# A fourth seven-product unit per column group in a gated MLP, with part of the weight preparation done by adding transfers

## The chip, the cores and the metric

The kernel runs on one core of one Trainium2 chip. The metric is the device time of one execution in microseconds (us). A core has a matrix engine (TensorE, "PE" in the profile, its weight loads "PEld"), VectorE ("DVE"), ScalarE ("ACT"), GpSimd ("POOL") and SyncE ("SP"). Transfers are issued from the queues of SP, POOL or ACT and carried by 16 DMA engines.

## The reference

One layer of an encoder over 256 rows of width 2048, all in float32: four mixers side by side, a cross-attention to 256 memory rows, and a gated MLP of width 5632, which is where nearly all of the change lies.

```python
def swiglu(h, w_gate_up, w_down):
    gate, up = jnp.split(h @ w_gate_up, 2, axis=-1)
    return (jax.nn.silu(gate) * up) @ w_down

# in reference():
    x = x + mix @ w_out[l]
    x = x + cross_attention(rms_norm(x, norm_g[l, 1]), mem_n, w_xq[l], w_xkv[l], w_xo[l])
    x = x + swiglu(rms_norm(x, norm_g[l, 2]), w_gate_up[l], w_down[l])
return rms_norm(x, final_norm_g)
```

`w_gate_up` is 2048 x 11264 and `w_down` 5632 x 2048.

## The kernel before

**Precision.** Every large product is made of three: an operand is split into a high part, rounded to the matrix engine's shorter float32 format (`F32R`), and a low part, the rest. High x high, high x low and low x high are added up in PSUM (`part`, lines 489 to 493, whose three matmuls are the profile's lines L490, L491 and L492).

**The stream of weights** (`class Stream`). All weights come in one host-packed tensor `W`, in the order of use, in slabs of 128 x 2048 (1 MB). `raw` issues a slab's load on SP's queue (L134) into one of three raw buffers; gate and up have a fourth (`rawx`). `make` prepares the next half slab of 1024 columns: `split` has ScalarE copy it into `wh` (L154) and VectorE subtract that copy from it into `wl` (L155). `look` prepares as many halves ahead as there are buffers (`free`): three pairs of `wh` and `wl` in the pool `wp`, and two more in `wp2` during gate and up, five in all, one of them being in use. When TensorE has used a half up, `drop` gives its buffer back.

**Gate and up** (`gate_up`). The 5632 columns are worked off in eleven groups j of 512 gate and 512 up columns. The depth 2048 is cut into eight slabs i per group, each two blocks of 128 deep by the two column sets. A plain slab is 24 matmuls of 512 columns: two blocks, two column sets, two halves of the 256 rows, three products each. A "seven-product" slab (`seven`, `sevens`, `unit`) treats the same data as a 2 x 2 by 2 x 2 block product and forms it with seven block products in place of eight (Strassen's scheme in Winograd's form), so 21 matmuls. For that, sums and differences of the blocks are needed: those of the activations are formed once, before the first group (`left`, in the tiles `sh` and `sl`), and those of the weights for each slab by VectorE in the raw buffer (`make`, L187). Such a slab is prepared in four parts:

- part 0: split of 512 columns, then one subtraction over 1024;
- part 1: split of 1024, then two sums over 512;
- parts 2 and 3: splits of 1024 of what now stands in the raw buffer.

Of four accumulators, p1, p5, p6 and p7, `combine` makes the unit's share of the four results after the group's last unit; `finish` adds the plain part, applies the SiLU and the product in the next group, and `store_turned` transposes the gated product (L520) and stores it to the DRAM tensor `hidden` in four transfers per half of the rows (L525), from which `fetch` (L936) later reloads it for the product with `w_down`. In the same stage `turn` transposes the residual (L1069), stores it to `xrows` (L1072), and loads it back in row order.

Numbers such as "slab 2" or "unit 5" below are i in a group; "second half" is part 1 of a plain slab.

**Order.** Side work runs as generators (`Background`): `poll` steps one on when its time has come and an account of VectorE's work (`owed`, increased by `bg.dve` and paid off by `bg.pe`) is low. The program is written in one order, but each engine's queue is put in order by a planner ahead of time, by priority and by its own estimate of when operands are ready. `keep_place` (`keep` in the stream) pins instructions behind the one that precedes them in the program on the same engine. In `make` the parts of seven-product slabs are pinned, those of plain slabs are not. An engine runs its queue strictly in that order.

At the start the keys of the cross-attention are made (`mixers`, the loop over `w_xkv`): the first pass makes 1024 columns in step with the arriving input, two more passes 512 each; all their turned stores go through `store_turned(..., True)`, which pins the transposes.

Of the kernel before, what the change touches and what calls it, by code (L numbers as in the profile page):

```python
# [18 lines left out]
ALU = mybir.AluOpType  # L19
# [30 lines left out]

def sevens(j):

    return (1, 3, 5) if j else (5,)


FORMED = 6
# [50 lines left out]
PI_LO = float(np.nextafter(np.float32(math.pi), np.float32(0)))  # L107


class Stream:  # L110


# [32 lines left out]
                return pool  # L145
        return None

    def split(self, pool, at, r, edges):

        nc = self.nc  # L150
        wh, wl = (pool.tile([P, 1088], F32R, name=t, tag=t) for t in ("wh", "wl"))
        wh, wl = wh[:, at:at + 1024], wl[:, at:at + 1024]
        for a, b in zip(edges, edges[1:]):
            nc.scalar.copy(wh[:, a:b], r[:, a:b])  # L154
            nc.vector.tensor_tensor(out=wl[:, a:b], in0=r[:, a:b], in1=wh[:, a:b].bitcast(F32), op=ALU.subtract)  # L155
        self.bg.dve(edges[-1], len(edges) - 1)
        self.items.append((pool, wh, wl))

    def make(self):

        nc, (slab, part) = self.nc, self.todo
        n = 16 * slab + 8 * part
        if n >= NBLK - HELD:
            parts = [(self.places.pop(0)) for _ in range(2)]
            r = self.raw(slab)[:, part * 1024:part * 1024 + 1024]
            for a, (wh, wl) in zip((0, 512), parts):
                nc.scalar.copy(wh, r[:, a:a + 512])
                nc.vector.tensor_tensor(out=wl, in0=r[:, a:a + 512], in1=wh.bitcast(F32), op=ALU.subtract)
            self.bg.dve(1024, 2)
            self.items.append((None, parts))  # L170
            self.todo = (slab + part, 1 - part)
            return True
        pool = self.free(slab)
        if pool is None:
            return False
        raw = self.raw(slab)
        at = 48 if any(a <= n < b for a, b in ROWS) else 8
        r = raw[:, part % 2 * 1024:part % 2 * 1024 + 1024]
        if not seven(slab):
            mark = len(nc.cur_bb.bb.instructions)  # L180
            self.split(pool, at, r, [0, 256, 512, 1024] if n == 0 else [0, 512, 1024] if n == 8 else [0, 1024])
            if DOWN <= slab < DOWN + 2 * AHEAD:
                self.keep(mark)
            self.todo = (slab + part, 1 - part)
            return True
        mark = len(nc.cur_bb.bb.instructions)
        op = lambda out, a, b, what=ALU.subtract: nc.vector.tensor_tensor(out=out, in0=a, in1=b, op=what)  # L187
        self.split(pool, at, r, [0, 512] if part == 0 else [0, 1024])
        b11, b12, b22, b21 = (raw[:, a:a + 512] for a in range(0, 2048, 512))
        if part == 0:  # L190
            blk = raw.rearrange("p (b c) -> p b c", b=4)
            op(r.rearrange("p (b c) -> p b c", b=2), blk[:, 0:3:2, :], blk[:, 1:2, :].to_broadcast([P, 2, 512]))
            self.bg.dve(1024)
        elif part == 1:
            op(b22, b22, b11, ALU.add)
            op(b21, b21, b22)
            self.bg.dve(1024, 2)
        self.keep(mark)
        self.todo = (slab + part // 3, (part + 1) % 4)
        return True  # L200
# [87 lines left out]
class Block:  # L288
# [223 lines left out]
                    self.bg.poll()  # L512
        return ps

    def store_turned(self, to, u, src, keep=False):

        nc = self.nc
        self.bg.dve(src.shape[1])
        mark = self.mark()
        nc.vector.transpose(u, src)  # L520
        if keep:
            self.keep_place(mark)
        to = to.rearrange("(b f) t -> f b t", f=32)
        for a in range(4):
            nc.gpsimd.dma_start(to[:, :, 32 * a:32 * a + 32],  # L525
                                u[32 * a:32 * a + 32, :].rearrange("f (b t) -> f b t", t=32))


# [46 lines left out]
    def mixers(self):  # L575
# [77 lines left out]
        with tc.tile_pool(name="mid", bufs=1) as mid:  # L653
            self.dgp = mid
            gl = Gla(self, mid)
            with tc.tile_pool(name="hyp", bufs=1) as hyp, tc.tile_pool(name="k2", bufs=8) as k2:
                hy = Hyena(self, hyp, k2)

                mem0 = hy.piece()[:, 0:R + 16]
                nc.sync.dma_start(mem0, self.t["mem0"])  # L660
                self.bg.add(prepare(mid))

                for cols in ([0, 512], [1024], [1536]):
                    first = dict(parts=[[k] for k in range(KT)], before=start_m) if len(cols) > 1 else {}
                    for c, ps in zip(cols, self.gemm_rows("w_xkv", cols, h, **first)):
                        for r in range(2):
                            self.store_turned(self.kd[c:c + 512, r * P:(r + 1) * P], hy.piece(), ps[r][:, :], True)
                    if first:
                        for k in range(0, KT, 4):
                            self.load_x(k, 4)  # L670
                for hd in range(4):
                    for r, p in enumerate(self.gemm_rows("w_xkv", [D + hd * 512], h, start_x if hd == 3 else rows.append)[0]):
                        for c in range(2):
                            v, o = self.tmp(), (2 * hd + r) * 512 + c * R
                            nc.scalar.activation(v, p[:, c * R:(c + 1) * R], AF.Copy, scale=self.rcm[:, r:r + 1])
                            nc.gpsimd.dma_start(self.vd[:, o:o + R], v)
                self.bg.drain()

                def ev_u(i, p):
                    hy.feed(i, self.merge(p))  # L680
                    if i == 4:
                        self.bg.add(hy.convs())

                self.gemm("w_in", [UH + i * P for i in range(12)], h, ev_u)
                for r, p in enumerate(self.gemm_rows("w_in", [512], h, lambda k: k or low_rank())[0]):
                    nc.scalar.copy(gl.v[r], p)
                self.gemm("w_in", [256, 384, 0, 128], h, lambda i, p: gl.feed(i, self.merge(p)))
                self.gemm("w_in", scols[0:NSC], h, ev_s, narrow=True)
                self.bg.drain()
# [261 lines left out]
    def gate_up(self, sw, gp, f):  # L951
# [8 lines left out]

        def left():

            for i in (5, 1, 3):
                t = [self.tmp() for _ in range(2)]
                for x, k in zip(t, (2 * i, 2 * i + 1)):
                    nc.scalar.activation(x, self.resk(k), AF.Copy, scale=self.gvec(V_NG + 32, k))
# [37 lines left out]
        def finish(j, cs, s):  # L1004
# [9 lines left out]
            for r in range(2):  # L1014
                g, h = s[r]
                u = gp.tile([P, 512], F32, name="u", tag="u", bufs=2)
                self.stt(h, h, box["col"][:, r:r + 1], g, ALU.mult, ALU.mult)
                yield SOON
                self.store_turned(self.ff[j * 512:(j + 1) * 512, r * P:(r + 1) * P], u, h)
                yield SOON  # L1020
            self.stored.append(j)

# [39 lines left out]
    def turn(self):  # L1062
# [3 lines left out]
        for i in range(16):  # L1066
# [2 lines left out]
            nc.vector.transpose(u, self.resk(i))  # L1069
            for a in range(4):  # L1070
                c = i * P + 32 * a
                nc.gpsimd.dma_start(to[:, :, c:c + 32], u[32 * a:32 * a + 32, :].rearrange("t (b f) -> t b f", f=32))  # L1072
            yield 4.0
        for c in range(4):
            for r in range(2):
# [783 lines left out]
```

## Time and profile before

| | |
|---|---|
| time, median of 3 runs | 1458.29 us (1456.57 to 1458.53) |
| the profiled execution | 1457.18 us, its span 1455.3 us |
| PE busy | 1440.2 us, 99% |
| DVE busy | 1192.2 us, 82% |
| ACT busy | 844.1 us, 58% |
| POOL busy | 172.2 us, 12% |
| moved by transfers | 307.16 MB, 211 GB/s on the mean |

The span is that of one execution taken by the hardware profiler; the profiled time contains 1.9 us around it. Matmuls overlap: one of 512 columns lasts 389 ns in the records, and the next starts before it has ended, so the spacing of starts and not the duration counts. In a row of groups the columns are the line and engine, the operation, what it writes and reads, the count, the busy time with the mean in ns, and the idle time before it with what ended it. In the DMA rows the last number is the median from issue to landing. Gate and up take about 755 to 1210 us of the span.

### The profile page before, as it was taken

What the parts mean: (1) busy time and instruction counts of PE and PEld (TensorE: products, weight loads), DVE (VectorE), ACT (ScalarE), POOL (GpSimd) and SP (SyncE); (2) the same over time, 40 slices, a digit from 0 to 9 for tenths busy, and PEclk for the clock granted to TensorE, in tenths of its full rate; (3) what the DMA queues carried; (4) which work ended last, traced back from release to release, by engine and by line L of the source; (5) the groups of instructions that cost most, each with busy time, mean ns of one, the idle gap of its engine ahead of it and who ended that gap; (6) DMA issues with size and microseconds to landing.
All of it is one profiled execution on the core that took longest, in us unless ns stands there. A gap on an engine that the chain in (4) does not pass through costs nothing.

```text
span 1455.3 us, 19732 instructions
## 1 busy us (share of the span) xinstructions
PE 1440.2 (99%) x7219; PEld 1217.8 (84%) x7219; DVE 1192.2 (82%) x1748; ACT 844.1 (58%) x1252; POOL 172.2 (12%) x294
## 2 busy tenths in 40 slices
PE   9999999999999999999999999999999999999997
PEld 7788888888899888888888888888888888788886
DVE  6577768777868867877778999999999997988875
ACT  6466665456646656665555565555555654655554
POOL 0220100000000001110003334112111112100000
PEclk9999999999999999999999999999999999999999
DMA  9885654444535555555556767656667656545554
GB/s 351 283 314 192 229 193 169 174 158 167 206 122 203 204 200 203 185 174 177 199 191 221 252 234 245 241 191 244 234 228 248 207 198 235 216 183 200 224 203 145
DMA packets 57394, 307.16 MB, mean 211 GB/s; under 512 B 9774, under 2 KB 11471, under 8 KB 25681
## 3 DMA queue, kind: packets, MB, share of 16 engines
q1 hardware_dynamic: 45920, 281.11, 54.2%
q0 software_dynamic: 10944, 24.14, 5.5%
q8 instruction: 56, 0.92, 0.2%
q10 hardware_dynamic: 432, 0.66, 0.1%
q14 instruction: 42, 0.34, 0.1%
HBM read 291.71 MB, written 14.16 MB: 210 GB/s over the span
## 4 chain that ended last, share of the span: by engine, by line
PE 96%; DVE 2%; ACT 1%; issue 0%; DMA 0%; SPq 0%; ACTq 0%; DVEq 0%
PE pg L439 19%; PE pg L490 13%; PE pg L491 13%; PE pg L492 13%; PE pg L440 10%; PE pm L490 7%; PE pm L492 7%; PE pm L491 7%; PE pm L1360 1%; DVE wl L155 1%; PE pg L436 1%; PE pg L437 1%; PE pm L890 1%; PE pm L863 1%; ACT wh L154 0%
## 5 line engine op out<-in xcount | busy, mean ns | idle before, releaser
L154 ACT CAST wh<-raw 128x1024 fp32r<-128x1024 f32 (+1 forms) x589 | 589.2, 1013 | 473.1 <-PE pg L492 147.3
L155 DVE TENSOR_TENSOR wl<-raw,wh 128x1024 fp32r<-128x1024 f32 (+1 forms) x589 | 681.8, 1176 | 183.7 <-ACT wh L154 178.0
L439 PE MATMUL pg<-act,wh 128*128 128x512 f32 x1104 | 387.5, 393 | 0.0
L440 PE MATMUL pg<-act,wl 128*128 128x256 f32 x1216 | 340.7, 280 | 0.0
L490 PE MATMUL pg<-wh,act 128*128 128x512 f32 (+1 forms) x689 | 269.6, 392 | 2.3 <-DVE k L520 2.0
L491 PE MATMUL pg<-wl,act 128*128 128x512 f32 (+1 forms) x689 | 268.8, 390 | 1.2 <-DVE wl L155 1.1
L492 PE MATMUL pg<-wh,act 128*128 128x512 f32 (+1 forms) x689 | 268.8, 390 | 0.0
L439 PEld LDWEIGHTS pg<-act,wh 128*128 128x128 f32 x1104 | 207.4, 188 | 45.0
L440 PEld LDWEIGHTS pg<-act,wl 128*128 128x128 f32 x1216 | 228.5, 188 | 0.8 <-DVE wl L155 0.5
L490 PEld LDWEIGHTS pg<-wh,act 128*128 128x128 f32 x689 | 129.7, 188 | 31.0 <-ACT dgh L410 2.4
L491 PEld LDWEIGHTS pg<-wl,act 128*128 128x128 f32 x689 | 129.6, 188 | 29.2 <-DVE wl L155 2.5
L492 PEld LDWEIGHTS pg<-wh,act 128*128 128x128 f32 x689 | 129.7, 188 | 27.3
L491 PE MATMUL pm<-wl,act 128*128 128x512 f32 x318 | 123.7, 389 | 0.0
L492 PE MATMUL pm<-wh,act 128*128 128x512 f32 x318 | 123.7, 389 | 0.0
L490 PE MATMUL pm<-wh,act 128*128 128x512 f32 x318 | 123.6, 389 | 0.0
L187 DVE TENSOR_TENSOR raw<-raw 128x1024 f32<-128x1024 f32 x129 | 111.8, 866 | 3.0
L525 POOL DMA_DIRECT2D hidden<-u x88 | 56.8, 653 | 164.6 <-DVE u L520 141.9
L492 PEld LDWEIGHTS pm<-wh,act 128*128 128x128 f32 x318 | 59.7, 188 | 12.5
L491 PEld LDWEIGHTS pm<-wl,act 128*128 128x128 f32 x318 | 59.7, 188 | 12.4
L490 PEld LDWEIGHTS pm<-wh,act 128*128 128x128 f32 x318 | 59.7, 188 | 12.4
L1072 POOL DMA_DIRECT2D xrows<-tmp x64 | 37.0, 585 | 183.5 <-DVE rc L321 126.6
L936 POOL DMA_DIRECT2D tmp<-hidden x44 | 24.5, 560 | 141.2 <-DVE f L317 73.0
(353 smaller groups left out, 1773.1 us busy)
## 6 DMA issues: line engine op xcount, KB each, us to landing
raw<-in_W SPq DMA_DIRECT2D x246, 1024.0 KB, 4.9
raw<-in_W SPq DMA_DIRECT2D x11, 512.0 KB, 7.5
hidden<-u POOLq DMA_DIRECT2D x88, 64.0 KB, 4.4
tmp<-hidden POOLq DMA_DIRECT2D x44, 128.0 KB, 4.2
res<-in_xT SPq DMA_DIRECT2D x8, 512.0 KB, 7.5
k<-in_mem SPq DMA_DIRECT2D x8, 256.0 KB, 6.5
k<-in_x SPq DMA_DIRECT2D x8, 256.0 KB, 7.7
keys<-k POOLq DMA_DIRECT2D x32, 64.0 KB, 5.3
```

Of the source, the lines that this page charges most:

```text
L154: nc.scalar.copy(wh[:, a:b], r[:, a:b])
L155: nc.vector.tensor_tensor(out=wl[:, a:b], in0=r[:, a:b], in1=wh[:, a:b].bitcast(F32), op=ALU.subtract)
L187: op = lambda out, a, b, what=ALU.subtract: nc.vector.tensor_tensor(out=out, in0=a, in1=b, op=what)
L436: self.nc.tensor.matmul(p[:, 0:R], wh, slot[:, 0:R], start=start, stop=False)
L439: self.nc.tensor.matmul(p[:, :], wh, slot[:, :], start=start, stop=False)
L440: self.nc.tensor.matmul(p[:, 0:R], wl, slot[:, 0:R], start=False, stop=stop)
L490: self.nc.tensor.matmul(p, hi, wh, start=start, stop=False)
L491: self.nc.tensor.matmul(p, hi, wl, start=False, stop=False)
L492: self.nc.tensor.matmul(p, lo, wh, start=False, stop=stop)
L525: nc.gpsimd.dma_start(to[:, :, 32 * a:32 * a + 32], u[32 * a:32 * a + 32, :].rearrange("f (b t) -> f b t", t=32))
L936: self.nc.gpsimd.dma_start(m[k], self.ff[k * P:(k + 1) * P, :])
L1072: nc.gpsimd.dma_start(to[:, :, c:c + 32], u[32 * a:32 * a + 32, :].rearrange("t (b f) -> t b f", f=32))
```

## The change

Four things change.

1. In groups j = 1 to 10, slab 4 becomes a fourth seven-product slab: units are now slabs 1, 3, 4 and 5, so three follow each other. `left` forms the activation sums for slab 4 too. Group 0 keeps its single unit.
2. In those groups the second half of each plain slab (0, 2, 6, 7) is split in another way (`added`): ScalarE writes the negated rounding of the raw half into `wl`, a transfer on POOL's queue adds the raw half to it, and ScalarE copies the rounding into `wh`. VectorE takes no part.
3. The stores of the gated product and of the turned residual go on SP's queue and not on POOL's.
4. In the first pass of the keys the transposes are no longer pinned; in the other passes they are.

```diff
--- before.py
+++ after.py
@@ -50,7 +50,7 @@
 
 def sevens(j):
 
-    return (1, 3, 5) if j else (5,)
+    return (1, 3, 4, 5) if j else (5,)
 
 
 FORMED = 6
@@ -105,6 +105,12 @@
 TWO_PI_3 = float(2 * math.pi - 6.28125 - float(np.float32(2 * math.pi - 6.28125)))
 MAGIC = float(np.float32(1.5 * 2 ** 23))
 PI_LO = float(np.nextafter(np.float32(math.pi), np.float32(0)))
+
+
+def added(slab):
+
+    j, i = divmod(slab - GU // 16, 8)
+    return j >= 1 and slab < DOWN and i not in sevens(j)
 
 
 class Stream:
@@ -145,11 +151,17 @@
                 return pool
         return None
 
-    def split(self, pool, at, r, edges):
+    def split(self, pool, at, r, edges, added=False):
 
         nc = self.nc
         wh, wl = (pool.tile([P, 1088], F32R, name=t, tag=t) for t in ("wh", "wl"))
         wh, wl = wh[:, at:at + 1024], wl[:, at:at + 1024]
+        if added:
+            nc.scalar.mul(wl, r, -1.0)
+            nc.gpsimd.dma_start(wl, r.bitcast(F32R), accum_op=ALU.add)
+            nc.scalar.copy(wh, r)
+            self.items.append((pool, wh, wl))
+            return
         for a, b in zip(edges, edges[1:]):
             nc.scalar.copy(wh[:, a:b], r[:, a:b])
             nc.vector.tensor_tensor(out=wl[:, a:b], in0=r[:, a:b], in1=wh[:, a:b].bitcast(F32), op=ALU.subtract)
@@ -178,7 +190,7 @@
         r = raw[:, part % 2 * 1024:part % 2 * 1024 + 1024]
         if not seven(slab):
             mark = len(nc.cur_bb.bb.instructions)
-            self.split(pool, at, r, [0, 256, 512, 1024] if n == 0 else [0, 512, 1024] if n == 8 else [0, 1024])
+            self.split(pool, at, r, [0, 256, 512, 1024] if n == 0 else [0, 512, 1024] if n == 8 else [0, 1024], part == 1 and added(slab))
             if DOWN <= slab < DOWN + 2 * AHEAD:
                 self.keep(mark)
             self.todo = (slab + part, 1 - part)
@@ -512,7 +524,7 @@
                     self.bg.poll()
         return ps
 
-    def store_turned(self, to, u, src, keep=False):
+    def store_turned(self, to, u, src, keep=False, queue=None):
 
         nc = self.nc
         self.bg.dve(src.shape[1])
@@ -522,7 +534,7 @@
             self.keep_place(mark)
         to = to.rearrange("(b f) t -> f b t", f=32)
         for a in range(4):
-            nc.gpsimd.dma_start(to[:, :, 32 * a:32 * a + 32],
+            (queue or nc.gpsimd).dma_start(to[:, :, 32 * a:32 * a + 32],
                                 u[32 * a:32 * a + 32, :].rearrange("f (b t) -> f b t", t=32))
 
 
@@ -664,7 +676,7 @@
                     first = dict(parts=[[k] for k in range(KT)], before=start_m) if len(cols) > 1 else {}
                     for c, ps in zip(cols, self.gemm_rows("w_xkv", cols, h, **first)):
                         for r in range(2):
-                            self.store_turned(self.kd[c:c + 512, r * P:(r + 1) * P], hy.piece(), ps[r][:, :], True)
+                            self.store_turned(self.kd[c:c + 512, r * P:(r + 1) * P], hy.piece(), ps[r][:, :], not first)
                     if first:
                         for k in range(0, KT, 4):
                             self.load_x(k, 4)
@@ -960,7 +972,7 @@
 
         def left():
 
-            for i in (5, 1, 3):
+            for i in (5, 1, 3, 4):
                 t = [self.tmp() for _ in range(2)]
                 for x, k in zip(t, (2 * i, 2 * i + 1)):
                     nc.scalar.activation(x, self.resk(k), AF.Copy, scale=self.gvec(V_NG + 32, k))
@@ -1016,7 +1028,7 @@
                 u = gp.tile([P, 512], F32, name="u", tag="u", bufs=2)
                 self.stt(h, h, box["col"][:, r:r + 1], g, ALU.mult, ALU.mult)
                 yield SOON
-                self.store_turned(self.ff[j * 512:(j + 1) * 512, r * P:(r + 1) * P], u, h)
+                self.store_turned(self.ff[j * 512:(j + 1) * 512, r * P:(r + 1) * P], u, h, queue=nc.sync)
                 yield SOON
             self.stored.append(j)
 
@@ -1069,7 +1081,7 @@
             nc.vector.transpose(u, self.resk(i))
             for a in range(4):
                 c = i * P + 32 * a
-                nc.gpsimd.dma_start(to[:, :, c:c + 32], u[32 * a:32 * a + 32, :].rearrange("t (b f) -> t b f", f=32))
+                nc.sync.dma_start(to[:, :, c:c + 32], u[32 * a:32 * a + 32, :].rearrange("t (b f) -> t b f", f=32))
             yield 4.0
         for c in range(4):
             for r in range(2):
```

## The prediction

> **What bounds the kernel now.** I read the busy table, the slices and the chain of the page first.
>
> ```profile
> span 1455.3 us, 19732 instructions
> PE 1440.2 (99%) x7219; PEld 1217.8 (84%) x7219; DVE 1192.2 (82%) x1748; ACT 844.1 (58%) x1252; POOL 172.2 (12%) x294
> ...
> DVE  6577768777868867877778999999999997988875
> ...
> PE 96%; DVE 2%; ACT 1%; issue 0%; DMA 0%; SPq 0%; ACTq 0%; DVEq 0%
> ```
>
> TensorE carries the chain, so a matmul less is time less, as long as what feeds it keeps up. But VectorE's slices stand at 9 from about the 23rd to the 33rd: that is gate and up, the stage that changes. The busy table of 800 to 1200 us (PE, PEld, DVE, ACT, POOL, clock, DMA share, GB/s) says how near VectorE is:
>
> ```profile
> 800.00:1200.00 400.00, 400.00 (x1767) 331.20 (x1766) 381.40 (x438) 227.51 (x257) 91.70 (x150) 1.00 0.66 229
> ```
>
> TensorE has no gap in 400 us; VectorE is 95% busy, ScalarE 57%, the DMA engines 66%. So there is a second bound 5% behind the first. The waits of the stage show what sets the pace of the weight preparation:
>
> ```profile
> ACT wh L154 <- PE pg L492: 66.9, 55, 2.1
> ACT wh L154 <- PE pm L492: 58.7, 46, 6.2
> DVE wl L155 <- ACT wh L154: 24.3, 25, 3.5
> ...
> SPq L134 <- DVE wl L155: 384.8, 78, 10.7
> ```
>
> ScalarE waits until TensorE has given a buffer back: the preparation runs five half slabs ahead and cannot run further. SP's queue spends most of its time waiting for a raw buffer, so it has room.
>
> **Step 1, the matmuls.** Starts of the first matmuls of units 3 and 5 of one column group (start, duration):
>
> ```profile
> 893.24 0.39 PE L491 MATMUL pm<-wl,act 128*128 128x512 f32 x1
> ...
> 895.74 0.39 PE L490 MATMUL pg<-wh,act 128*128 128x512 f32 x1
> ...
> 905.93 0.39 PE L490 MATMUL pg<-wh,act 128*128 128x512 f32 x1
> ```
>
> Between the last two lie unit 3 (21) and plain slab 4 (24): 45 matmuls in 10.19 us, 0.2264 each; the 0.39 overlaps. The new unit drops 3 of 24 in each of ten groups: 30 x 0.2264 = -6.8 us, exposed.
>
> **Step 2, VectorE.** Its rows of that stretch give the spacing (the stretch holds plain and seven-product work, and two of the turned residual's transposes), and the groups the counts:
>
> ```profile
> 894.80 5.37 DVE L155 TENSOR_TENSOR wl<-raw,wh 128x1024 fp32r<-128x1024 f32 x5
> ...
> 902.49 0.44 DVE L1069 STREAM_TRANSPOSE tmp<-res 128x256 f32<-128x256 f32 x1
> 902.85 1.38 DVE L187 TENSOR_TENSOR raw<-raw 128x512 f32<-128x512 f32 x2
> ...
> 912.52 1.22 DVE L155 TENSOR_TENSOR wl<-raw,wh 128x1024 fp32r<-128x1024 f32 x1
> 913.65 0.68 DVE L317 TENSOR_TENSOR h<-pg,m 128x512 f32<-128x512 f32 x1
> 914.25 0.68 DVE L317 TENSOR_TENSOR g<-pg,m 128x512 f32<-128x512 f32 x1
> ```
>
> An operation of 1024 takes 1.13 us of the engine (913.65 - 912.52), one of 512 takes 0.60, a background transpose 0.36. A plain slab is two long ones, 2.26. A seven-product slab is three long splits, one long subtraction, a short split and two short sums: 4 x 1.13 + 3 x 0.60 = 6.32. The new unit adds 4.06 a group; four second halves taken off return 4.52. On the mean VectorE gains 0.46 us, while TensorE's group shrinks by 0.68. The mean fits; the order does not. Units 3, 4 and 5 now follow each other, each 6.32 us of VectorE against 21 x 0.2264 = 4.75 of TensorE, and a lead cannot be saved up: the first part of unit 4 gets its buffer only when slab 2 is done, at 895.74 in these rows. With ScalarE's copy and the first split it stands at about 897.0; without a pause VectorE then finishes the third part of unit 5 10.9 us later (5.7 for the rest of unit 4, 5.2 in unit 5), near 907.95. TensorE wants it at 895.74 + 9.5 + 9 x 0.2264 + 0.23 = 907.5. That is 0.45 late, ten times: +4.5. Bounds: 0 if the planner begins earlier, 1.2 a group if two transposes of 0.36 fall among the units, as they do here.
>
> **Step 3, the adding transfers.** For a second half ScalarE writes the negated rounding, POOL issues a transfer that adds the raw half, ScalarE copies the high part. No such transfer is in the trace. The nearest rows, in the stage:
>
> ```profile
> 885.78 2.66 ACT L154 CAST wh<-raw 128x1024 fp32r<-128x1024 f32 x3 [1.39 <-PE pm L492]
> ...
> L154 ACT CAST wh<-raw 128x1024 fp32r<-128x1024 f32 x186 | 190.9, 1049 | 153.7 <-DVE raw L187 69.6 <-PE pm L492 43.3 <-PE pg L492 38.3
> ...
> raw<-in_W SPq DMA_DIRECT2D x77, 1024.0 KB, 5.2
> ...
> tmp<-hidden POOLq DMA_DIRECT2D x24, 128.0 KB, 4.6
> res<-xrows POOLq DMA_DIRECT2D x6, 256.0 KB, 4.1
> ...
> L936 POOL DMA_DIRECT2D tmp<-hidden x44: 546/556/582, 817.0 to 1257.5; - x44
> ...
> DMA to landing us min/median/max: 3.4/4.8/7.2
> ```
>
> It writes 512 KB and has 512 KB of source and as much of destination to read, so I take the 1024 KB row, 5.2, plus POOL's 0.55 of issuing: about 5.8 us. Ends: 4.1 (256 KB on POOL's queue) and 7.2 (the slowest of those eight).
>
> By the Trainium skill, "DMA: Bandwidth & Descriptors" (Anatomy of one DMA), a transfer from GpSimd costs 2.0 us plus bytes over 436 GB/s; for 1024 KB an estimate of 4.4, by which this step would cost nothing in the next paragraph. For 256 KB the same fit gives 2.6 where the rows above have 4.1 to 4.8, so the trace does not bear it out.
>
> Slab 2: its first half is cast from 885.78, the negation of its second half follows at 886.8 to 887.8 (a copy of ScalarE is 1.05), and TensorE's first use of that low part is the matmul at 893.24. Budget 5.4: at 5.8 it is 0.4 late, +4 in ten groups (0 at 4.1, +18 at 7.2). Slab 6, behind three units: its first half and its negation stand in ScalarE's list near the last cast of unit 5, which needs VectorE's sums to be ready, at 906.8. In program order the negation ends at 909.9, lands at 915.7, and is wanted at 895.74 + 3 x 4.75 + 12 x 0.2264 + 0.23 + 0.45 = 913.4: 2.3 late. Put ahead of that cast, the transfer is nearly in time, but the cast comes 1 us later and unit 5's fourth part is 0.7 late. The planner orders plain halves by its own estimate of readiness (only the unit's instructions are pinned), so I take the 0.7: +7 (0 to +23). Slabs 7 and 0 have one to three us more. ScalarE's extra work, four negations and one and a half casts a group, is 5.5 x 1.05 = 5.8 us in a group of 41 where at 57% it idles 17: hidden.
>
> **Step 4, queues.** POOL loses 88 and 64 stores:
>
> ```profile
> POOL hidden L525 <- DVE u L520: 141.9, 10, 31.3
> ...
> POOL tmp L936 <- DMA hidden<-u: 22.6, 4, 6.9
> ...
> L525 POOL DMA_DIRECT2D hidden<-u x88: 648/648/677, 804.9 to 1221.8; - x88
> ```
>
> They waited 141.9 us there for transposes, and the adding transfers would have stood behind them. What stays on POOL and can still hold them up is the reload of the gated product, 4 waits of up to 6.9. On SP a store waits for the same VectorE queue that releases the raw buffers of the loads behind it, so it comes in their order; at 0.65 each (POOL's row; SP has none of short runs) 152 stores are 99 us of the 384.8 that SP waits. Raw loads are three slabs ahead, some 15 us against 5.2: cost 0, and a few us if a store holds a load longer than that.
>
> **Step 5, keys.** The first turned stores lose their pin, at TensorE's one long gap:
>
> ```profile
> 50.78 1.23 DVE L155 TENSOR_TENSOR wl<-raw,wh 128x1024 fp32r<-128x1024 f32 x1
> 51.92 2.50 DVE L520 STREAM_TRANSPOSE k<-pg 128x512 f32<-128x512 f32 x4
> ...
> 52.78 0.54 PE L490 MATMUL pg<-wh,act 128*128 128x512 f32 x1 [1.99 <-DVE k L520]
> ...
> 56.50 0.40 PE L490 MATMUL pg<-wh,act 128*128 128x512 f32 x1
> ...
> 1258.40 0.50 PE L491 MATMUL pg<-wl,act 128*128 128x512 f32 x1 [0.87 <-DVE wl L155]
> 1258.74 0.40 PE L492 MATMUL pg<-wh,act 128*128 128x512 f32 x1
> ...
> 1259.20 0.40 PE L491 MATMUL pg<-wl,s 128*128 128x512 f32 x1
> ```
>
> A gap of 1.99, and then nine matmul spacings in 3.72 us instead of 2.04: the clock fell for a while, 1.7 more. After the gap of 0.87 near the end it did not (two spacings in 0.46 from 1258.74). If the transposes pass the split of 50.78 the gap is about 0.9 and the fall goes: -2.8. If the planner leaves them, 0. I take -2.0; the ends are -3.7 and 0.
>
> The Trainium skill, "TensorE: Matmul & The Clock Gate" (Why this matters for your kernels), asks for no gaps over about 3 us; the 1.99 here already cost speed, so the trace is stricter. By the rule no wait of steps 2 and 3 could cost more than itself; by this row one of 2 us can.
>
> The sixth pair of forms for unit 4 (eight small VectorE and ScalarE operations) falls before 780 us, where TensorE waits for nothing: 0.
>
> **Sum**: -6.8 + 4.5 + 4 + 7 - 2.0 = +6.7. The profiled execution took 1457.18 (span 1455.3 and 1.9 around it), 1.1 under the median 1458.29; on the median this is **1465.0 us**.
>
> **Rivals.**
> 1. The transfers land in time (4.1 to 4.6, as all smaller POOL rows do) and the planner hides the third unit: -6.8 - 2.8 and at most +4.5, so 1449 to 1454, middle 1451. For it: size hardly shows between 128 and 256 KB. Against: 66% DMA load and a doubled read. Chance 0.36.
> 2. They land in time, but a background transpose falls among the units: (0.45 + 0.36) x 10 = 8.1 against 8.8: 1457.6, no change. Chance 0.13.
> 3. The second half of slab 6 stays in program order, 2.3 late, and each such gap also drops the clock as at 52.78 (1.7): 4.0 a group instead of 0.7, +33: 1498. It decides from a gap somewhere between 0.87 and 1.99 us. Chance 0.07.
>
> The forecast has 0.44 with its own range 1459 to 1482 (transfers landing at 5.4 and step 5 at -3.7: +1.0; at 7.2 and step 5 at 0: +22.7). The range 1450 to 1485 takes in three quarters of case 1 and some of the forecast's tail; a quarter of case 1, case 3 and a few hundredths of that tail lie outside, not quite 0.2.
>
> **What would show it.** Right: low parts by adding transfers at 5 to 6 us to landing; TensorE waiting in gate and up, for VectorE's low part in units 4 and 5 and for a transfer in slabs 2 and 6, 1.0 to 2 us a group in all; VectorE below 95% there. Wrong: TensorE without gaps from 800 to 1200 us (rival 1), landings under 4.6 or over 7.2, or the stage held by raw loads that come late behind SP's stores. The gap at 52 us shows step 5 alone.

## The result and the profile after

The changed kernel takes **1552.15 us** (median of 4, 1549.23 to 1555.46) against 1457.43 in the same comparison: a ratio of **1.0653** (95% interval 1.0639 to 1.0667), about 95 us slower. The forecast was 1465 and the range ended at 1485. All ratios below are against the kernel before, and 0.001 is 1.46 us.

The page of the changed kernel, its span, busy table and the head of its chain:

```profile
span 1548.7 us, 19931 instructions
...
PE 1466.7 (95%) x7189; PEld 1222.6 (79%) x7189; DVE 1194.7 (77%) x1763; ACT 894.7 (58%) x1315; POOL 113.6 (7%) x182
...
DVE  6687768869587678777877887778687777898885
...
PE 73%; DMA 12%; issue 8%; DVE 5%; ACT 1%; POOL 1%; SPq 0%; POOLq 0%; ACTq 0%; DVEq 0%
```

TensorE has the 30 matmuls less (7189), yet is busy 26.5 us longer, and idle for 1548.7 - 1466.7 = 82.0 us where it was idle for 15.1. DMA has come into the chain with 12%, and VectorE's nines of gate and up are now sevens and eights: it was not VectorE that became the bound. The same 400 us as in the prediction (PE, PEld, DVE, ACT, POOL, clock, DMA share, GB/s):

```profile
800.00:1200.00 400.00, 349.02 (x1430) 275.96 (x1429) 314.82 (x369) 225.49 (x256) 41.01 (x55) 0.96 0.81 233
```

TensorE went from 400 to 349 us of 400, the granted clock from 1.00 to 0.96. What it waits for over the whole program (total, times, longest; L502 and L503 are `part`'s first two matmuls here, L160 the negation, L161 the transfer, L162 the copy):

```profile
PE pm L503 <- DMA wl<-raw: 28.6, 10, 4.9
PE pg L503 <- DMA wl<-raw: 28.1, 11, 6.1
PE pg L503 <- DVE wl L167: 5.7, 9, 1.1
PE pg L502 <- ACT wh L166: 2.8, 6, 0.8
PE pm L503 <- DVE wl L167: 2.6, 4, 1.3
PE pm L502 <- ACT wh L166: 2.2, 4, 0.9
```

56.7 us in 21 waits are for the adding transfers, two in nearly every group, and 13.3 us in 23 short waits for VectorE and ScalarE. Read one transfer at a time, ten of the 21 are at slab 2 (19.4 us), seven at slab 6 (30.2), three at slab 7 and one at slab 0. The DMA issues (KB each, median us to landing), and the transfer's own line:

```profile
raw<-in_W SPq DMA_DIRECT2D x246, 1024.0 KB, 5.1
wl<-raw POOLq DMA_DIRECT2D x40, 512.0 KB, 7.9
...
DMA to landing us min/median/max: 4.7/7.9/11.5
```

512 KB inside the chip take 7.9 us where 1024 KB from memory take 5.1. That median is a mixture: slab 2's transfers land in 6.1 us on the median and slab 6's in 6.6, while slab 7's and 0's, mostly issued a few microseconds behind slab 6's, take about 9 and make TensorE wait only four times. One such wait at slab 6, in the timeline (start, duration):

```profile
927.57 1.05 ACT L162 CAST wh<-raw 128x1024 fp32r<-128x1024 f32 x1
...
928.52 1.05 ACT L160 ACTIVATE wl<-raw 128x1024 fp32r<-128x1024 f32 x1
...
929.87 0.90 POOL L161 DMA_DIRECT2D wl<-raw  x1 [16.83 <-DVE m L329]
...
935.93 0.50 PE L503 MATMUL pm<-wl,act 128*128 128x512 f32 x1 [2.95 <-DMA wl<-raw]
```

and one at slab 2:

```profile
949.77 1.05 ACT L166 CAST wh<-raw 128x1024 fp32r<-128x1024 f32 x1 [2.44 <-PE pg L504]
950.73 1.04 ACT L162 CAST wh<-raw 128x1024 fp32r<-128x1024 f32 x1
951.81 0.62 ACT L166 CAST wh<-raw 128x512 fp32r<-128x512 f32 x1
952.34 1.06 ACT L160 ACTIVATE wl<-raw 128x1024 fp32r<-128x1024 f32 x1
953.69 0.86 POOL L161 DMA_DIRECT2D wl<-raw  x1 [17.28 <-DVE tmp L1081]
...
959.86 0.50 PE L503 MATMUL pg<-wl,act 128*128 128x512 f32 x1 [2.46 <-DMA wl<-raw]
```

In both, ScalarE takes the copy of line 162 (and at slab 2 another cast, of 512 columns) ahead of the negation of line 160, on which the transfer depends. TensorE wanted the low part at 932.98 and 957.40.

A wait costs more than itself. Around the one of 808.45:

```profile
806.00 0.39 PE L502 MATMUL pm<-wh,act 128*128 128x512 f32 x1
808.45 0.71 PE L503 MATMUL pm<-wl,act 128*128 128x512 f32 x1 [2.06 <-DMA wl<-raw]
808.96 0.63 PE L504 MATMUL pm<-wh,act 128*128 128x512 f32 x1
...
811.94 0.42 PE L502 MATMUL pm<-wh,act 128*128 128x512 f32 x1
```

Eight spacings take 3.49 us (808.45 to 811.94) instead of 8 x 0.2264 = 1.81: the clock fell (granted 0.64 from 808 to 810, 0.51 from 810 to 812). After the wait at 935.93 it did not, though it was longer (granted 1.00 from 936 to 940):

```profile
936.26 0.39 PE L504 MATMUL pm<-wh,act 128*128 128x512 f32 x1
936.49 0.40 PE L503 MATMUL pm<-wl,act 128*128 128x512 f32 x1
```

Eleven of the 21 waits are followed by such a fall. Added up in steps of half a microsecond, the speed that was not granted behind them comes to 21.8 us.

### The profile page after: what moved, and what is told of

It reads as the page before. It is cut to its first block, busy times and chain, and to the rows that moved or that the text cites. A ratio compares the mean times of both kernels' runs of the same rounds, so it can differ in the third digit from the quotient of the medians.

```text
span 1548.7 us, 19931 instructions
## 1 busy us (share of the span) xinstructions
PE 1466.7 (95%) x7189; PEld 1222.6 (79%) x7189; DVE 1194.7 (77%) x1763; ACT 894.7 (58%) x1315; POOL 113.6 (7%) x182
## 3 DMA queue, kind: packets, MB, share of 16 engines
q0 software_dynamic: 11840, 37.24, 10.3%
## 4 chain that ended last, share of the span: by engine, by line
PE 73%; DMA 12%; issue 8%; DVE 5%; ACT 1%; POOL 1%; SPq 0%; POOLq 0%; ACTq 0%; DVEq 0%
PE pg L451 17%; PE pg L503 10%; PE pg L504 10%; DMA wl<-raw 10%; PE pg L452 9%; PE pg L502 9%; PE pm L503 4%; PE pm L504 3%; PE pm L502 3%; DVE wl L167 2%; DMA raw<-in_W 2%; DVE raw L199 1%; PE pm L1372 1%; ACT wh L166 1%; PE pg L448 1%
## 5 line engine op out<-in xcount | busy, mean ns | idle before, releaser
L166 ACT CAST wh<-raw 128x1024 fp32r<-128x1024 f32 (+2 forms) x569 | 565.1, 1003 | 502.9 <-PE pg L504 158.4
L167 DVE TENSOR_TENSOR wl<-raw,wh 128x1024 fp32r<-128x1024 f32 (+2 forms) x569 | 656.9, 1165 | 257.3 <-ACT wh L166 250.8
L503 PE MATMUL pg<-wl,act 128*128 128x512 f32 (+1 forms) x664 | 265.5, 400 | 29.4 <-DMA wl<-raw 28.1
L504 PE MATMUL pg<-wh,act 128*128 128x512 f32 (+1 forms) x664 | 263.4, 397 | 0.0
L502 PE MATMUL pg<-wh,act 128*128 128x512 f32 (+1 forms) x664 | 257.9, 395 | 0.1
L503 PEld LDWEIGHTS pg<-wl,act 128*128 128x128 f32 x664 | 128.1, 193 | 61.8 <-DMA wl<-raw 32.7
L504 PEld LDWEIGHTS pg<-wh,act 128*128 128x128 f32 x664 | 128.0, 193 | 27.2 <-issue 0.4
L502 PEld LDWEIGHTS pg<-wh,act 128*128 128x128 f32 x664 | 126.5, 191 | 28.7 <-ACT wh L166 1.4
L503 PE MATMUL pm<-wl,act 128*128 128x512 f32 x293 | 119.9, 409 | 28.6 <-DMA wl<-raw 28.6
L199 DVE TENSOR_TENSOR raw<-raw 128x1024 f32<-128x1024 f32 x159 | 137.6, 865 | 3.7
L504 PE MATMUL pm<-wh,act 128*128 128x512 f32 x293 | 118.2, 404 | 0.0
L502 PE MATMUL pm<-wh,act 128*128 128x512 f32 x293 | 114.7, 399 | 0.0
L503 PEld LDWEIGHTS pm<-wl,act 128*128 128x128 f32 x293 | 57.1, 195 | 44.9 <-DMA wl<-raw 32.8
L504 PEld LDWEIGHTS pm<-wh,act 128*128 128x128 f32 x293 | 57.7, 197 | 12.2
L502 PEld LDWEIGHTS pm<-wh,act 128*128 128x128 f32 x293 | 56.7, 194 | 13.0 <-ACT wh L166 0.7
L161 POOL DMA_DIRECT2D wl<-raw x40 | 35.1, 877 | 280.5 <-ACT wl L160 158.0
L160 ACT ACTIVATE wl<-raw 128x1024 fp32r<-128x1024 f32 x40 | 42.3, 1056 | 1.4 <-PE pg L503 1.4
L162 ACT CAST wh<-raw 128x1024 fp32r<-128x1024 f32 x40 | 41.6, 1040 | 0.5 <-PE pg L504 0.3
```

The lines of the kernel that those rows point to most:

```text
L160: nc.scalar.mul(wl, r, -1.0)
L161: nc.gpsimd.dma_start(wl, r.bitcast(F32R), accum_op=ALU.add)
L162: nc.scalar.copy(wh, r)
L502: self.nc.tensor.matmul(p, hi, wh, start=start, stop=False)
L503: self.nc.tensor.matmul(p, hi, wl, start=False, stop=False)
L504: self.nc.tensor.matmul(p, lo, wh, start=False, stop=stop)
```

## The experiments

The theory after the result: TensorE waits for adding transfers that land late, and this is nearly all of the loss. The rivals: the stores on SP hold up the raw loads; three units in a row starve TensorE; the transfers take DMA time from the raw loads.

**no_add**, the changed kernel without the transfer (the low part is left as the negated rounding):

```
             nc.scalar.mul(wl, r, -1.0)
-            nc.gpsimd.dma_start(wl, r.bitcast(F32R), accum_op=ALU.add)
             nc.scalar.copy(wh, r)
```

> The changed kernel without the adding transfers: ScalarE still writes the negated rounding and the copy, but the low part stays the negated rounding (that part of the computation is left out). Theory A (the transfers land after TensorE wants the low part, and each late one also drops the clock): the 56.7 us of waits for them and some 33 us of slower matmuls go, and what is left is the saved matmuls (-6.8), the removed gap at the keys (-3.7) and up to 10 us of waits for VectorE and ScalarE behind the three units in a row: 1447 to 1457 us. Theory B (the stores on SP's queue hold up the raw loads or fill the DMA engines, and the transfers only show it): the raw loads then are late themselves, TensorE waits for the copies instead, over 1480 us. Theory C (three units in a row overload VectorE): over 1465 us with waits for VectorE's low parts.

Measured: 1473.67, ratio 1.0115 (1.0102 to 1.0129). So the transfers carry 1.0653 - 1.0115 = 0.0538, **78 us of the 95**. In the profiled spans (1548.7 and 1472.4) these are 51.5 us of TensorE's idle time and 24.8 of a longer busy time (1466.7 against 1441.9), most of it the 21.8 us of lower clock (the mean granted clock is 0.983 against 0.998). The time lies above the 1447 to 1457 that I expected if the transfers were nearly all of the loss, and in the range of three units in a row overloading VectorE (over 1465): both theories hold a part. What is left here stands in units 4 and 5, TensorE's waits of one group:

```profile
1073.40 0.50 PE L501 MATMUL pg<-wh,sh 128*128 128x512 f32 x1 [0.92 <-ACT wh L165]
...
1078.19 0.50 PE L502 MATMUL pm<-wl,sh 128*128 128x512 f32 x1 [1.10 <-DVE wl L166]
...
1080.79 0.51 PE L502 MATMUL pg<-wl,sh 128*128 128x512 f32 x1 [0.93 <-DVE wl L166]
```

**stores_pool**, the changed kernel with both stores back on GpSimd's queue (at lines 1031 and 1084):

```
-  ..., u, h, queue=nc.sync)       nc.sync.dma_start(to[:, :, c:c + 32], ...
+  ..., u, h)                      nc.gpsimd.dma_start(to[:, :, c:c + 32], ...
```

> The changed kernel with the stores of the gated product and of the turned residual on POOL's queue again. On SP's queue they made 61,000 more packets of 128 bytes and the DMA share of the stage went from 0.66 to 0.82. Theory A with packets as its cause: fewer packets, the transfers land in about 6 us instead of 7.9, the waits fall by 1.5 to 2 us each at some 21 places: 1490 to 1525 us. Theory A with the transfer's own length as its cause: landing stays at 7 to 8 us, and the stores' waits for transposes now stand ahead of transfers on POOL's queue: 1545 to 1575 us.

Measured: 1561.73, ratio 1.0725 (1.0705 to 1.0745), landing 4.5/6.5/12.2 (least, median, most). With transfers on GpSimd's queue the move is right, by 0.0072; the transfers are late with or without it. I had tied this time to an unchanged landing, but the landing is shorter here: TensorE waits less for transfers (40.4 us in 16 waits) and more for VectorE and ScalarE (34.0 in 39 against 13.3 in 23).

**stores_only**, the kernel before with just the stores moved (the converse of that edit, made in the kernel before):

> The kernel before with only the stores moved to SP's queue. If the packets fill the DMA engines or the stores hold up the raw loads (theory B): 5 to 20 us slower, with ScalarE waiting for raw loads in gate and up. If the raw loads' lead of three slabs covers both (theory A): within 3 us of before, the DMA share of the stage up from 0.66 to about 0.72.

Measured: 1463.13, ratio 1.0040 (1.0026 to 1.0053): +6 us, where I had 0; that is in the range of the rival (5 to 20), whose sign, ScalarE waiting for a raw load in gate and up, shows once (1.7 us at 791.48). The packets of the kernel before, then of this one, and this one's line of gated stores:

```profile
DMA packets 57394, 307.16 MB, mean 211 GB/s; under 512 B 9774, under 2 KB 11471, under 8 KB 25681
```

```profile
DMA packets 116401, 307.16 MB, mean 210 GB/s; under 512 B 71213, under 2 KB 72910, under 8 KB 84688
...
L525 SPq DMA_DIRECT2D hidden<-u x88: 302/498/2387, 804.0 to 1223.3; - x88
```

The same bytes go in twice as many packets. An issue takes 0.498 us on the median, less than the 0.65 on GpSimd's queue, but up to 2.387. Which of the two makes the 6 us was not tried. Little of it stands in gate and up: TensorE has one wait there, 1.1 us for VectorE's split at 912.79, and from 1200 to 1300 us it waits 4.1 us where the kernel before waits 1.8.

**keys_only**, the kernel before with just the keys' stores unpinned:

```
-  self.store_turned(self.kd[...], hy.piece(), ps[r][:, :], True)
+  self.store_turned(self.kd[...], hy.piece(), ps[r][:, :], not first)
```

> The kernel before with only the first keys' transposes unpinned. The gap of 1.99 us at 52 us and the slower matmuls behind it (1.7 us) go: 3.7 us faster, about 1453.7 us. Rival: the clock falls at another place of the start, so that only the gap is won: 2 us; or nothing, if the input's transfers set the pace there.

Measured: 1453.44, ratio **0.9975** (0.9966 to 0.9984), which beats both kernels. Its rows at the former gap:

```profile
49.74 2.08 DVE L520 STREAM_TRANSPOSE k<-pg 128x512 f32<-128x512 f32 x3
...
51.74 2.32 DVE L155 TENSOR_TENSOR wl<-raw,wh 128x1024 fp32r<-128x1024 f32 x2
...
52.26 0.39 PE L490 MATMUL pg<-wh,act 128*128 128x512 f32 x1
```

The transposes now run ahead of the split, and the matmul at 52.26 waits for nothing: the gap has gone, and the fall of the clock with it.

**far**, the changed kernel with transfers only at slabs 0 and 7 (`i in (0, 7)` in place of `i not in sevens(j)`), VectorE making the low parts of slabs 2 and 6:

> The changed kernel with adding transfers only for the second halves of slabs 7 and 0; those of slabs 2 and 6, just behind units, go back to VectorE. Without any transfer the changed kernel took 1473.7 us; VectorE gets 2.26 us a group more. Theory A (a transfer costs only where its time to landing is over its lead; 7 and 0 have leads of about 8 to 11 us): waits for transfers nearly vanish, and VectorE, at about 41.3 us a group, holds the stage: 1475 to 1495 us. Rival (transfers one after another slow each other and the raw loads whatever their lead): slab 0's transfer stays late, over 1510 us.

Measured: 1526.14, ratio 1.0474 (1.0457 to 1.0492), landing 7.9/9.4/10.7. That is in the range of the rival (over 1510), but the late slab is not the 0 that it named. With half the transfers, TensorE still waits 27.3 us for them in 10 waits, and all ten are at slab 7: TensorE wants its low part 4.9 to 8.4 us after the issue (landing less wait), and it lands after 8.3 to 10.7. Slab 0's transfers land in 7.9 to 10.3 and are in time, so a long enough lead does help; slab 7's is under the 8 to 11 that I had given it. (VectorE does two more subtractions a group, so this is no pure half of the 78.)

**pinned**, the changed kernel with the negation, the transfer and the copy kept in program order:

```
+            mark = len(nc.cur_bb.bb.instructions)
             nc.scalar.mul(wl, r, -1.0)
...
+            self.keep(mark)
```

> The changed kernel with the negation, the transfer and the copy of an added half pinned to their place in the program, so that the negation no longer stands behind copies that the planner put ahead of it (1.6 us at slab 2, 1 us at slab 6). If ScalarE's order is a main part of the lateness: 1 to 2 us less at some 20 places, 1510 to 1530 us. If the transfer's own length is (7.9 to landing against leads of 5 to 6): 1540 to 1555 us.

Measured: 1548.54, ratio 1.0615 (1.0580 to 1.0649); TensorE waits 49.4 us for transfers, landing 7.1 on the median. The waits at slab 2 fall from 19.4 to 14.3 us, those at slab 6 stay (30.7). The planner's order of ScalarE is worth some 4 to 6 us, and the two intervals overlap.

**three_add**, the changed kernel with units 1, 3 and 5 only, so five transfers a group:

```
-    return (1, 3, 4, 5) if j else (5,)
+    return (1, 3, 5) if j else (5,)
```

> The changed kernel without the fourth unit: units are slabs 1, 3 and 5, and the second halves of slabs 0, 2, 4, 6 and 7 are made by adding transfers. VectorE has 5.7 us a group less than before, so nothing is left of its bound. Theory A: slabs 2, 4 and 6 each come behind a unit with a lead of about 5.4 from the end of the negation, so three late transfers a group instead of two to three, with falls of the clock: 1535 to 1575 us, although VectorE and TensorE both have room. Rival (the loss is made by three units in a row, which throw ScalarE's and VectorE's order late, and the transfers only follow): under 1490 us.

Measured: 1545.23, ratio 1.0601 (1.0585 to 1.0617), with 51.1 us of waits for transfers. VectorE is at 272 of 400 us here, so neither its load nor the fourth unit is what makes the transfers late.

**four_dve**, the other half: four units, no transfer (`added` returns False), stores on GpSimd's queue, and VectorE makes every low part:

> The fourth unit alone (and the unpinned keys): no adding transfers, stores on POOL's queue as before; VectorE makes all low parts. Its work a group is then about 39.3 + 4.1 = 43.4 us against 40.75 of TensorE's: if VectorE holds the stage, ten groups of 43.4 to 44 instead of 41.4, less 3.7 for the keys: 1473 to 1482 us, VectorE at 97% or more from 800 to 1200 us. Rival (three units in a row cost more than VectorE's sum, as in the run without transfers, 1.7 us of waits a group beside it): 1485 to 1500 us.

Measured: 1492.52, ratio 1.0235 (1.0219 to 1.0250). That is the range that I had given to the rival, that three units in a row cost more than VectorE's sum: VectorE is at 385 of 400 us, hardly above the 381 of the kernel before, and TensorE waits 19.7 us for ScalarE's and 11.0 for VectorE's parts. So a fourth unit alone loses 34 us, and with the transfers the loss is larger still.

Then the transfer by itself. **scratch_add** is keys_only with 40 adding transfers into spare tiles that nobody reads:

```
+            to = self.spare[self.turn % len(self.spare)]
+            self.turn += 1
+            nc.gpsimd.dma_start(to[:, :1024], r[:, :1024], accum_op=ALU.add)
```

> Leaves out the fourth unit and the stores' move: keys_only, plus 40 adding transfers of 512 KB from the raw second halves of slabs 0, 2, 6 and 7 of each group into two spare tiles, which TensorE never reads (VectorE still makes the low parts that are used). A raw buffer is given back only when its transfer has landed. Theory A (the transfer is slow in itself under this stage's load, and its cost lies in TensorE waiting for it): landing near the 7.9 us of the changed kernel, time within 6 us of keys_only's 1453. Theory B (the transfers take DMA time from the raw loads, and that holds up the stage): waits of TensorE spread over the units too, 1470 or more. Theory C (it was late because it stood behind other work of its own preparation): landing under 6 us.

**scratch_copy** is the same without `accum_op`:

> As scratch_add, but each of the 40 transfers is a plain copy and not an addition. Leaves out the fourth unit and the stores' move. If the addition makes it slow: landing at 5 us or less, against 7 to 8 in scratch_add. If it is the load of the queues or the size: landing within 1 us of scratch_add's.

**scratch_half** adds 512 columns, 256 KB:

> As scratch_add, but each transfer takes 512 of the 1024 columns (256 KB) into one of four spare tiles. If the time of a transfer is mostly bytes: landing about 2 us shorter than scratch_add's. If it is mostly fixed, or waiting behind raw loads in the DMA engines: within 1 us of it.

Measured: 1453.71, 1453.19 and 1453.21, ratios 0.9977, 0.9976 and 0.9969 (intervals of 0.0012 or less to either side): all three are keys_only's time. Their DMA rows, in that order:

```profile
spare<-raw POOLq DMA_DIRECT2D x40, 512.0 KB, 9.5
```

```profile
spare<-raw POOLq DMA_DIRECT2D x40, 512.0 KB, 5.5
```

```profile
spare<-raw POOLq DMA_DIRECT2D x40, 256.0 KB, 5.8
```

And 800 to 1200 us of keys_only, scratch_add and scratch_copy:

```profile
800.00:1200.00 400.00, 400.00 (x1766) 331.24 (x1765) 381.36 (x437) 227.74 (x257) 91.75 (x150) 1.00 0.67 232
```

```profile
800.00:1200.00 400.00, 400.00 (x1766) 331.25 (x1765) 381.62 (x437) 227.36 (x256) 126.88 (x188) 1.00 0.92 280
```

```profile
800.00:1200.00 400.00, 400.00 (x1767) 331.20 (x1766) 381.63 (x438) 228.48 (x257) 112.79 (x188) 1.00 0.79 281
```

Three things follow. Contention falls as a rival in the form that transfers starve the raw loads: with the DMA engines at 92% and a raw buffer held until its transfer has landed, TensorE still has no gap. (That the raw loads lengthen the transfers is not excluded by this.) The adding is what makes it slow: 9.5 against 5.5 us for the same bytes at the same places. And the DMA time of the added bytes doubles: the share rises by 0.25 for adding and by 0.12 for copying, at 280 and 281 GB/s. The Trainium skill, "Collectives: The Full Stack" (The bandwidth ceiling: the fold count and why AG ≠ RS ≠ AR), says of the reducing collectives that it isn't the addition that costs, but the second source that each chunk has to read through the same ring; the doubled share here agrees.

**copy_for_add** keeps every dependence of the changed kernel and takes the adding away (the low part is then the raw half itself):

```
-            nc.gpsimd.dma_start(wl, r.bitcast(F32R), accum_op=ALU.add)
+            nc.gpsimd.dma_start(wl, r.bitcast(F32R))
```

> The changed kernel with its 40 adding transfers made plain copies of the raw half (so the low part that is used is the raw half itself; the computation is wrong in that). Everything waits as before. If the length of the adding transfer is what made them late: landing about 5.5 us (7.9 in the changed kernel), waits for transfers under 15 us in all (56.7 there), time 1476 to 1495. If it is the place (negation behind other work of ScalarE, no lead at slabs 2 and 6): 1520 or more.

Measured: 1510.08, ratio 1.0374 (1.0354 to 1.0394), between the two cases. Its waits of TensorE, and its landing:

```profile
PE pg L503 <- DMA wl<-raw: 17.0, 9, 4.4
PE pm L503 <- DMA wl<-raw: 13.0, 10, 3.0
```

```profile
DMA to landing us min/median/max: 2.9/5.5/11.0
```

Of the 78 us, 1.0653 - 1.0374 = 0.0279, 41 us, are what adding costs over copying; the other 1.0374 - 1.0115 = 0.0259, 38 us, are there even at the 5.5 us of a copy. I had expected 1476 to 1495 for such a landing, with under 15 us of waits; there are 30.0. At slabs 2 and 6 the copies land in 5.0 and 4.8 us on the mean.

Last, what is left of no_add. **pairs_no_add** is no_add with units 1, 2, 4 and 5 (the plain slabs are then 0, 3, 6 and 7; `left` is changed to match):

```
-    return (1, 3, 4, 5) if j else (5,)
+    return (1, 2, 4, 5) if j else (5,)
```

> no_add with its units in slabs 1, 2, 4 and 5 in place of 1, 3, 4 and 5, so that never three follow each other; the low parts of the plain second halves (now slabs 0, 3, 6 and 7) are left as the negated rounding, as there. If three units in a row cost no_add its time: 1450 to 1460, with half of its waits for VectorE and ScalarE or fewer. If any two units in a row cost the same, or it is the extra work of ScalarE: 1468 to 1480.

Measured: 1468.74, ratio 1.0082 (1.0067 to 1.0097), 5 us under no_add. **neg_only** is keys_only with ScalarE's extra work, but neither a fourth unit nor moved stores; VectorE leaves out the subtraction of those halves, and the low part stays the negated rounding:

> keys_only with three units as before; in slabs 0, 2, 6 and 7 of each group the low part of the second half is only ScalarE's negated rounding (no transfer, no subtraction by VectorE; the computation is wrong in that). No fourth unit, no moved stores. If ScalarE's extra work is hidden, as I predicted: 1451 to 1454. If it makes the high parts late (waits for ScalarE's wh in units): 1458 to 1466.

Measured: 1455.99, ratio 0.9998 (0.9989 to 1.0007), 3 us over keys_only's 0.9975 and between my two cases. But gate and up are not where they arise:

```profile
800.00:1200.00 400.00, 400.00 (x1767) 331.20 (x1766) 342.13 (x401) 263.40 (x298) 93.11 (x153) 1.00 0.68 233
```

TensorE has no gap there, as in keys_only. Its waits that are longer than in keys_only are one of 1.1 us in the first 200 us and 3.0 us (against 1.3) from 1230 to 1300 us. **no_add_pool** is no_add with the stores on GpSimd's queue:

> no_add (the changed kernel without the adding transfer; the low part is left as the negated rounding) with both stores back on GpSimd's queue. If the moved stores cost the same here as alone (stores_only, +6): 1466 to 1469. If they cost nothing beside the fourth unit: 1472 to 1475. If the fourth unit needs them moved: more than 1476.

Measured: 1469.58, ratio 1.0091 (1.0075 to 1.0108), so the moved stores cost 3.5 us beside the fourth unit; the two intervals overlap, and only stores_only shows that cost alone.

## Why the prediction was wrong, by its own steps

The runs give each term as a difference of two ratios, times 1457. The five differences form one chain of runs from the kernel before to the changed one, so that they add up to the whole by construction; what is measured is each one alone:

| Step | Predicted | Measured | From |
|---|---|---|---|
| 1 and 2, fourth unit (30 matmuls less, units in a row) | -6.8 + 4.5 | +13.6 | no_add_pool less neg_only |
| 3, transfers | +11 | +78 | changed less no_add |
| 3, ScalarE's extra work | 0 | +3.4 (none of it as a wait from 800 to 1200 us) | neg_only less keys_only |
| 4, queues | 0 | +3.5 (alone +5.8) | no_add less no_add_pool (stores_only) |
| 5, keys | -2.0 | -3.6 | keys_only |
| sum | +6.7 | +95 | changed: +95 |

**Step 3 is the one that failed**, by 67 us of the 88 that were missed, in three places.

First the landing: 5.8 was taken from the raw loads' row, with an upper end of 7.2; it is 7.9 on the median and up to 11.5. At the two slabs that the step had priced it is less far off, 6.2 (slab 2) and 6.9 us (slab 6) on the mean, with about 0.3 from the end of the negation to the issue. The step saw that an addition has two operands to read, and then priced it by a row of a plain load with as many bytes in all. Such a transfer costs twice the DMA time of a copy (scratch_add against scratch_copy), and no row of the kernel before had one. But the landing is not the whole of it: copy_for_add, landing below 5.8 on the mean at both slabs, still loses 38 us to transfers where the step had 11.

Second the budgets. At slab 6 the sum took the 0.7 us of a planner that puts the negation first. The trace shows the other case that the step had worked out, behind the unit's last cast as in program order (with the copy ahead of the negation, too): the negation ends at 929.57 and TensorE wants the low part at 932.98, a budget of 3.4, where that case had 913.4 - 909.9 = 3.5. At slab 2 the budget of 5.4 became 4.0 (953.40 to 957.40), since a copy and a 512-column cast went ahead of the negation; pinned shows that this order is worth little by itself. The waits are 1.9 us a group at slab 2 where the sum had 0.4, and 3.0 at slab 6 where it had 0.7. Slab 7, which the step had in time with one to three us more, is late in three groups.

Third, the waits were priced at their own length. The first, second and third together: 56.7 us of waits instead of 11, and some 25 of longer busy time, 21.8 of it the clock. **Rival 3 had the mechanism right for slab 6** (program order, late by over 2 us, the clock falling with it) and a chance of 0.07; its 1498 is still 54 us short, since it left slab 2 and the landing as they were. Rivals 1 and 2, transfers in time, had 0.49 and were wrong.

By the estimate of the Trainium skill, "DMA: Bandwidth & Descriptors" (Anatomy of one DMA), 4.4 us, the step would have cost nothing: the runs speak against it for a transfer under this load, with 9.5 us adding and 5.5 copying.

**Step 2 was mis-sized**, in the same way: 4.5 where some 20 are lost (13.6 + 6.8). "A lead cannot be saved up" seems to hold from the second unit on and not only at the third: with pairs, all but the 5 us between no_add and pairs_no_add remain. And its 0.45 a group was one wait; no_add_pool has 20 short ones in gate and up, 11.9 us, all in units' matmuls, where neg_only has none from 800 to 1200 us, and each costs more than its length. In the changed kernel the matmul after such a wait shows 0.50 in place of 0.39 and the next follows after 0.33 (935.93 to 936.26) in place of 0.2264. With the 0.39 - 0.2264 by which a matmul overlaps the next, that puts 0.16 + 0.10, about 0.3, beside each wait, so the 20 waits account for some 17 of the 20 us.

**Step 4 was mis-sized**: 0 where the stores on SP cost 4 to 6 us. The queue had the room that was seen: raw loads land in 5.0 us on the median with the stores on SP and without. On GpSimd's queue the gated stores wait 150.0 us for transposes in stores_pool, as the step had it, but what TensorE waits for longer there are VectorE and ScalarE and not the transfers. By what path the moved stores cost 4 to 6 us is open: the one raw load that ScalarE waits for in gate and up of stores_only (791.48) leaves TensorE without a gap.

**ScalarE's extra work** was called hidden, and from 800 to 1200 us of neg_only it is: ScalarE is busy for 263 of 400 us and TensorE has no gap. The 3 us that neg_only loses to keys_only stand at the start and behind gate and up, where the program is the same; that the planner's order shifted there is likely and not shown.

**Step 5 was right**, at its upper end of 3.7: both the gap and the clock's fall are gone.

**Step 1 was right in its count** (7189 matmuls); its gain is inside the first row of the table and doesn't show by itself.

What is open, except for a part, is why the landing of an adding transfer varies from 4.7 to 11.5 us in one kernel. The part that shows: in three_add slab 4's transfers, about ten microseconds or more from any other, land in 4.5 to 7.1 us, and slab 0's, behind those of slabs 6 and 7, in 6.7 to 11.1. But the first of the changed kernel, alone, took 9.0. A stretch of the DMA timeline without raw loads would tell, and wasn't tried.

## What to carry to other kernels

A transfer that takes over work of a busy engine has to be priced with its whole latency (from the end of what it waits for to landing) against the lead that its buffer allows, and the lead be read for the latest order that a planner may choose. If the next reader comes within that latency, bandwidth to spare doesn't help: here 40 transfers cost nothing without a reader, and 78 us with one. And price a short wait of a saturated TensorE at its length plus its restart, and one near 2 us or more at the clock's fall too: here it may come (after 1.80 and 2.06 us) or not (after 2.11 and 2.95), and behind every wait of 3.2 us and more of the changed kernel it came.

## What the runs showed of the hardware that I had not expected

- An adding transfer of 512 KB inside the chip takes 9.5 us to landing on the median where a copying one at the same places takes 5.5 (scratch_add and scratch_copy), and twice its share of the DMA engines (0.25 against 0.12). GpSimd's issue of it takes 0.9 us against 0.54 (0.86 to 0.90 in the rows above; copy_for_add's 40 issues have 0.537 to 0.546). 256 KB adding takes as long as 512 KB copying.
- The stores' short runs make one packet each from SP's queue and fewer on GpSimd's: 116,401 against 57,394 for the same bytes. Packets under 512 B rise by 61,439, and the 152 stores have 61,440 runs of 128 B; the larger packets fall by 2,432, 16 for each store.
- The clock's fall is not a matter of the gap's length alone, and it can begin late: behind the wait that ended at 889.00 (1.80 us) the granted clock stays at 1.00 for about 1.5 us and then stands at 0.50 for over 3 us. A wait of 2.06 us was followed by a fall, one of 2.95 by none. The Trainium skill, "TensorE: Matmul & The Clock Gate" (What's actually happening), says that activity is watched in a free-running window of about 3.4 us, so that it depends on where in the window a gap lies; these two rows agree with that better than with one threshold, which is how my prediction had put it.
